# Two transformer blocks on one core: the 512- and the 256-column products of four weight blocks are issued in groups of one length

## The chip, the cores and the metric

One core of one Trainium2 chip runs the whole program. The metric is the device time of one execution in microseconds, the median of several runs. Before the change it is 2228.6 us (three runs, 2227.95 to 2229.66).

## What is computed

Two transformer blocks follow each other on 256 tokens of width 2048, batch 1, all in f32. The first mixes a gated short convolution, trailing means and a cross attention to 256 memory rows; the second has a dilated and a differential attention. Each ends in a gated feed-forward with an inner width of 5632. Nearly all of the arithmetic is products of the 256 tokens with weight matrices:

```python
h = rmsnorm(x, g_mix[l]);  z = h @ w_in[l]          # 2048 x 3584
... conv, trailing means, cross attention ...
x = x + mix @ w_out[l]                              # 2048 x 2048
u = causal_dwconv(rmsnorm(x, g_ffn[l]) @ w_up[l], ffn_conv_w[l]) + ffn_conv_b[l]   # 2048 x 11264
gate, val = jnp.split(u, 2, axis=-1)
x = x + (jax.nn.silu(gate) * val) @ w_down[l]       # 5632 x 2048
... second block: w_in_2 (2048 x 6144), two attentions, w_out_2, w_gate_2, w_up_2, w_down_2 ...
```

## The kernel before

Each f32 value is split into two parts of 12 bits, an upper one (`hi`) and a lower one (`lo`), and a product is made as three products of parts: upper by upper, upper by lower, lower by upper. The activations lie in SBUF as `[upper 256 tokens | lower 256 tokens]`, 512 columns per row tile of 128 (`A`, `hid`, `mix`, `y`, `M`). The weights come in blocks of 128 x 128. For one block, the upper part of the weights is loaded into TensorE and the 512 columns move past it; then the lower part is loaded and only the first 256 columns, the upper halves, move past that. These are the two products of this text: the one of 512 columns (line 200, and line 203 for the last block of an output tile) and the one of 256 (line 201). Both add to one PSUM tile `acc` of 512 columns, the short one to its upper half. Each product has a weight load of its own.

`product` (from line 198) issues the two products of one block. For all blocks but the last of an output tile the long one goes first; for the last it is the short one, so that the long one closes the sum:

```python
def product(acc, hi, lo, x, first, last):
    if not last:
        nc.tensor.matmul(acc, lhsT=hi, rhs=x, start=first, stop=False)
    nc.tensor.matmul(acc[:, S:], lhsT=lo, rhs=x[:, :S], start=False, stop=False)
    if last:
        nc.tensor.matmul(acc, lhsT=hi, rhs=x, start=False, stop=True)
```

The weights come from HBM in units of 16 blocks (1 MB each, line 185's `raw`), and a unit is taken in four quarters of four blocks. `emit_all` (line 977 on) goes through the quarters in order. In each it puts out, in this order: the load of the unit three ahead (first quarter), half a unit's `split_hi` on ScalarE (line 173) and `split_lo` on VectorE (line 185) for the units to come, the work that follows on finished output tiles (`post`), the quarter's products, and then small products such as attention scores (`extra`). The schedule is manual, so each engine takes its instructions in the order in which they are written. `ws_units` makes the units in which the weights stand still: its `emit` goes through the four blocks of a quarter and calls `product`. An output tile of 16 row tiles is 16 blocks, which is just a unit; in the feed-forward's second and third part an output tile of `w_down` has 14. `full_blocks` and `late_order` give the order of blocks: the first two output tiles of a matrix leave their last two row tiles until both have all else. The products of `w_k` at the start are written out by themselves, four output tiles side by side, and call `product` too.

In `vs_unit` (lines 242 to 244) it is the activations that stand still and 512 columns of weights that move. There all products have 512 columns, three for each pair of row tile and half of the tokens.

Of the kernel before, what the change touches and what calls it, by code (L numbers as in the profile page):

```python
# [18 lines left out]
P = 128  # L19
# [40 lines left out]
def late_order(ms, ks, late=2):  # L60
    """(output tile, row tile) in the order in which they are multiplied: the first two output tiles
    leave the last row tiles, which are made last, until both have all else."""
    ms, ks = list(ms), list(ks)
    if not late:
        return [(m, k) for m in ms for k in ks]
    both = [(m, k) for part in (ks[:-late], ks[-late:]) for m in ms[:2] for k in part]
    return both + [(m, k) for m in ms[2:] for k in ks]
# [32 lines left out]
def tile_two_blocks(ctx: ExitStack, tc: tile.TileContext, a: dict, out: bass.AP):  # L100
# [35 lines left out]
    def post(t, fn):  # L136
        """fn is called in quarter t of the units' time, before its products; a generator's
        further stages come a quarter later each."""
        posts.setdefault(t, []).append(fn)

    def extra(t, fn):
        """fn is called in quarter t, behind its products."""
        extras.setdefault(t, []).append(fn)
# [21 lines left out]
    def split_hi(j):  # L165
        """Half a unit's weights as two parts of 12 bits: the upper one."""
        i, second = divmod(j, 2)
        c0 = HB * second
        if i >= len(units) or c0 >= units[i][1]:
            return  # L170
        n = min(units[i][1] - c0, HB)
        hi = whi_p.tile([P, HB], F32R, tag="hi", name=f"hi{j}")
        nc.scalar.activation(hi[:, :n], raws[i][:, c0:c0 + n], AF.Copy)  # L173
        halves[j] = (hi, None)

    def split_lo(j):
        """The lower one."""
        i, second = divmod(j, 2)
        c0 = HB * second
        if i >= len(units) or c0 >= units[i][1]:  # L180
            return
        n = min(units[i][1] - c0, HB)
        hi = halves[j][0]
        lo = wlo_p.tile([P, HB], F32R, tag="lo", name=f"lo{j}")
        nc.vector.tensor_tensor(out=lo[:, :n], in0=raws[i][:, c0:c0 + n], in1=hi[:, :n].bitcast(F32), op=ALU.subtract)  # L185
        halves[j] = (hi, lo)
# [10 lines left out]

    def product(acc, hi, lo, x, first, last):
        if not last:
            nc.tensor.matmul(acc, lhsT=hi, rhs=x, start=first, stop=False)  # L200
        nc.tensor.matmul(acc[:, S:], lhsT=lo, rhs=x[:, :S], start=False, stop=False)  # L201
        if last:
            nc.tensor.matmul(acc, lhsT=hi, rhs=x, start=False, stop=True)  # L203

    def ws_units(src, blocks, done, ready=0):
        """Weights stand still, the halves of 256 tokens move together: blocks of (tile, moving, first,
        last) in order. The sums are in two parts: by upper halves alone, and the rest."""
        accs = {}
        for u in range(0, len(blocks), UB):
            part = blocks[u:u + UB]  # L210

            def emit(i, q, part=part):
                for b, (m, mov, st, sp) in list(enumerate(part))[4 * q:4 * q + 4]:
                    if st:
                        accs[m] = acc_p.tile([P, 2 * S], F32, tag="acc", name="acc")
                    hi, lo = weights(i, b * P, (b + 1) * P)
                    product(accs[m], hi, lo, mov(), st, sp)

            i = add_unit(src[u // UB], len(part) * P, emit)
            for b, (m, _, _, sp) in enumerate(part):  # L220
                if sp:
                    post(max(4 * i + b // 4 + 1, ready), lambda m=m: done(m, accs.pop(m)))
# [7 lines left out]
    def vs_unit(src, act, g, accs):  # L230
        """Activations stand still, 512 columns of weights move: the unit of row tiles 4g to 4g + 3."""
        def emit(i, b):
# [22 lines left out]
    def rsqrt_small(src, n, scale, eps):  # L255
        """1 / sqrt(src * scale + eps), by columns of a few elements."""
        v = sm.tile([P, n], F32, tag=f"rs_v{n}", name="rs_v")
# [11 lines left out]
    class Norm:  # L269
        """rms of the tokens: sums of squares by partition, then r (token on partitions) and  # L270
        R (token along the row, the same on each partition)."""

# [35 lines left out]
        def rows(self, dst, r):  # L308
            """r[token] from partitions to the free axis, on all partitions."""
            for t in range(2):  # L310
# [6 lines left out]
        def at(self, t):  # L317
            """The last x is added in quarter t; R is there for the posts of the quarter returned."""
            extra(t + 4, self.sums)
# [5 lines left out]
    class TwoNorms(Norm):  # L325
        """A norm of x whose gained result is normed again: r and R serve both together, R1 the first."""

# [30 lines left out]
    def put_act(kt, g, x, a, norm):  # L358
        """x with its gain to the halves of a, and x itself to the norm."""
        hi = a[:, kt, :S]  # L360
# [6 lines left out]
    def put_pair(hl, src, scale=None):  # L367
        """The halves of hl add up to src (times a column of scales), the first of 12 bits."""
        h = hl[:, :S]
# [10 lines left out]
    def whole(acc):  # L380
        """The two parts of the sums as one, to be had from the next stage on."""
        z = t1.tile([P, S], F32, tag="t", name="z")
# [10 lines left out]

    # ---- attention: one head's scores to probabilities to [d, token] or [token, d]
    def scores(q, k, parts=(slice(0, P),)):
# [6 lines left out]
    def softmax(src, scale, normalise=True):  # L402
        """src [P, 2, S]: exp(scale * (src - max)) and 1 / its sums."""
        mx = sm.tile([P, 2], F32, tag="mx", name="mx")
# [25 lines left out]
    def transposed(p):  # L430
        """[token, key] to PSUM [key, key tile, token]."""
        ps = m_p.tile([P, 2, S], F32, tag="m", name="pT_ps")
# [9 lines left out]

    # ---------------------------------------------------------------- constants and first loads
    stg = big.tile([P, KT + KT * S], F32, tag="stg", name="mem")
# [9 lines left out]
    def first_units():  # L454
        """Loads and splits of mem and of the first two units, in the order in which the products take them."""
        n = 4 * P
        for i in range(3):
            raws[i] = wraw_p.tile([P, UB * P], F32, tag="raw", name=f"raw{i}")
            for q in range(4):
                if i != 1:  # L460
                    load_mem(2 * i + q, 2 * i + q + 1)
                nc.sync.dma_start(raws[i][:, q * n:(q + 1) * n], units[i][0][:, q * n:(q + 1) * n])
        # The tensor engine's clock rises with use: it is kept busy until the first operands are there.
        warm = m_p.tile([P, 512], F32, tag="m", name="warm")
# [39 lines left out]

    # ---------------------------------------------------------------- block 1: keys and values of mem
    n_mem = Norm("mem")
# [41 lines left out]
    for g in range(4):  # L548
        vs_unit(a["w_v"][g], lambda: M, g, v_accs)

        def emit(i, b, g=g):
            kt = 4 * g + b
            if kt == 0:
# [3 lines left out]
                for _ in range(2):  # L557
                    ac = s_p.tile([P, 2 * S], F32, tag="s", name="acc_s")
                    k_accs.append(ac)
            for m in range(4):  # L560
                hi, lo = weights(i, (4 * b + m) * P, (4 * b + m + 1) * P)
                product(k_accs[m], hi, lo, M[:, kt, :], kt == 0, kt == KT - 1)

# [12 lines left out]

    # ---------------------------------------------------------------- block 1: mixer
    mix = {}
# [40 lines left out]

    # trailing means  # L620
    pooled_hl = {}
# [38 lines left out]

    # gated short convolution
    conv = {}
# [43 lines left out]

    # ---------------------------------------------------------------- residual stream
    def residual(gname, norm, scaled_to=None):
# [28 lines left out]

    # ---------------------------------------------------------------- gated feed-forward
    hid = {}
# [41 lines left out]

    # ---------------------------------------------------------------- block 2: attention
    vv = {}
# [174 lines left out]

    # ---------------------------------------------------------------- emission
    def finish():  # L960
# [46 lines left out]

# ---- layouts: [units, 128, columns], each unit's rows as the tensor engine takes them
def _blocks(w, order):
    """The 128 x 128 blocks of w [K, N] in the order of (row tile, column tile) given."""  # L1010
    k, n = w.shape
# [4 lines left out]
def _units(blocks):  # L1016
    """[blocks, 128, 128] as units of 16."""
    n = -len(blocks) % UB
# [5 lines left out]
def _rows(w):  # L1024
    """w [2048, n] as [128, 16, n]."""
    return np.ascontiguousarray(w.reshape(KT, P, -1).transpose(1, 0, 2))


def _moving(w):
    """w [2048, 512 * n]: for each 512 columns, four units of four row tiles."""  # L1030
    n = w.shape[1] // 512
    return np.ascontiguousarray(w.reshape(4, 4, P, n, 512).transpose(3, 0, 2, 1, 4)).reshape(-1, P, 4 * 512)
# [66 lines left out]
```

## Time and profile before

| | |
|---|---|
| median of 3 runs | 2228.6 us |
| the profiled execution | 2228.2 us from the first to the last instruction |
| TensorE products, share of the span | 2208.6 us, 99% |
| TensorE weight loads | 1912.5 us, 86% |
| VectorE, ScalarE, GpSimd | 72%, 51%, 5% |
| DMA | 409 MB, mean 184 GB/s |
| blocks with a 512 and a 256 product | 5774 |

The profile gives each product's start and a modelled end. Products overlap in the array, so the time that one product costs is read from its start to the start of the next one, and not from its duration. In this text a step is that distance. "Long" is a product of 512 columns and "short" one of 256; long-to-short is the step from the start of a long product to that of a short one behind it.

### The profile page before, as it was taken

The page shows a single profiled execution, that of the slowest core. Times are in us where ns is not written, and L with a number is a line of the kernel's source. Part 1 is how long each engine was busy: PE and PEld are TensorE (multiplying, and loading weights), DVE is VectorE, ACT ScalarE, POOL GpSimd, SP SyncE. Part 2 cuts the span into 40 slices and gives each one's busy share as a digit, 9 for nine tenths or more (in the row PEclk, how much of TensorE's full clock was granted, in tenths as well). Part 3 has the DMA queues.
Part 4 walks back from the last instruction along what each step waited for, and adds up shares of the span by engine and source line. Part 5 has one row for each costly group of instructions (what it writes and reads, how often), then busy time and mean ns, then how long its engine had stood idle before and what let it go on. Part 6 is the DMA issues. An engine that isn't in the chain of part 4 may idle for free.

```text
span 2228.2 us, 31353 instructions
## 1 busy us (share of the span) xinstructions
PE 2208.6 (99%) x12426; PEld 1912.5 (86%) x12426; DVE 1604.0 (72%) x2553; ACT 1145.1 (51%) x1738; POOL 105.9 (5%) x114
## 2 busy tenths in 40 slices
PE   8999999999999999999999999999999999999997
PEld 7888888888888888888888888888888888888886
DVE  8877778885588757878779677776665666666666
ACT  6555546554455535565456655454443444344442
POOL 4000010000000000003100000010000000000012
PEclk9999999999999999999999999999999999999998
DMA  7555555555555555555554444555555555555553
GB/s 276 200 170 178 185 184 191 187 189 189 189 185 182 186 184 189 189 189 184 189 169 158 163 159 154 186 189 189 184 180 187 189 187 189 189 189 185 184 183 111
DMA packets 60196, 409.00 MB, mean 184 GB/s; under 512 B 6672, under 2 KB 8592, under 8 KB 11792
## 3 DMA queue, kind: packets, MB, share of 16 engines
q1 hardware_dynamic: 60048, 406.99, 53.2%
q8 instruction: 97, 1.59, 0.3%
q14 instruction: 51, 0.42, 0.0%
HBM read 404.86 MB, written 2.10 MB: 183 GB/s over the span
## 4 chain that ended last, share of the span: by engine, by line
PE 97%; DVE 2%; DMA 1%; issue 0%; ACT 0%; DVEq 0%; SPq 0%; ACTq 0%
PE acc L200 56%; PE acc L201 30%; PE acc L203 4%; PE acc L242 1%; PE acc L243 1%; PE acc L244 1%; PE s_ps L399 1%; DMA raw<-in_w_k 1%; DVE lo L185 1%; PE pT_ps L435 0%; PE o_ps L890 0%; PE o_ps L848 0%; DVE A L364 0%; DVE end L968 0%; DVE M L512 0%; DMA mem<-in_mem 0%
## 5 line engine op out<-in xcount | busy, mean ns | idle before, releaser
L200 PE MATMUL acc<-A,hi 128*128 128x512 f32 x3540 | 1267.5, 400 | 0.0
L173 ACT ACTIVATE hi<-raw 128x1024 fp32r<-128x1024 f32 x758 | 800.0, 1057 | 590.5 <-PE acc L200 342.2
L185 DVE TENSOR_TENSOR lo<-raw,hi 128x1024 fp32r<-128x1024 f32 x758 | 932.3, 1237 | 156.4 <-ACT hi L173 144.8
L201 PE MATMUL acc<-A,lo 128*128 128x256 f32 x3776 | 1021.7, 281 | 0.0
L200 PEld LDWEIGHTS acc<-A,hi 128*128 128x128 f32 x3540 | 665.2, 188 | 152.8 <-issue 1.7
L201 PEld LDWEIGHTS acc<-A,lo 128*128 128x128 f32 x3776 | 712.9, 189 | 22.8
L200 PE MATMUL acc<-hid,hi 128*128 128x512 f32 x1312 | 464.9, 395 | 0.0
L201 PE MATMUL acc<-hid,lo 128*128 128x256 f32 x1408 | 380.0, 281 | 0.0
L200 PEld LDWEIGHTS acc<-hid,hi 128*128 128x128 f32 x1312 | 246.7, 188 | 53.9
L201 PEld LDWEIGHTS acc<-hid,lo 128*128 128x128 f32 x1408 | 264.1, 188 | 8.8
L383 ACT ACTIVATE z<-acc 128x256 f32<-128x256 f32 x244 | 92.6, 382 | 298.4 <-PE acc L203 298.1
L385 DVE TENSOR_TENSOR z<-acc,z 128x256 f32<-128x256 f32 x244 | 103.3, 423 | 123.4 <-ACT z L383 121.0
L710 DVE TENSOR_TENSOR X<-acc,X 128x256 f32<-128x256 f32 x128 | 54.1, 422 | 172.7 <-PE acc L203 172.7
L203 PE MATMUL acc<-A,hi 128*128 128x512 f32 x236 | 94.2, 399 | 0.0
L685 DVE SCALAR_TENSOR_TENSOR c<-z,vec,c 128x255 f32<-128x255 f32 (+1 forms) x188 | 90.1, 481 | 4.6 <-ACT c L680 0.7
L373 DVE TENSOR_TENSOR hid<-hid 128x256 fp32r<-128x256 f32 x88 | 37.4, 425 | 73.5 <-ACT hid L371 73.5
L200 PE MATMUL acc<-mix,hi 128*128 128x512 f32 x240 | 85.1, 395 | 0.0
L200 PE MATMUL acc<-y,hi 128*128 128x512 f32 x224 | 80.7, 397 | 0.0
L391 DVE TENSOR_TENSOR z<-z,R_ffn 128x256 f32<-128x256 f32 x176 | 74.8, 425 | 6.0
L201 PE MATMUL acc<-mix,lo 128*128 128x256 f32 x256 | 69.4, 281 | 0.0
L201 PE MATMUL acc<-y,lo 128*128 128x256 f32 x256 | 66.6, 281 | 0.0
L286 POOL TENSOR_TENSOR sq_attn<-sq_attn,sqt 128x256 f32<-128x256 f32 x30 | 29.4, 992 | 717.4 <-ACT sqt L284 717.3
(188 smaller groups left out, 1577.8 us busy)
## 6 DMA issues: line engine op xcount, KB each, us to landing
raw<-in_w_up SPq DMA_DIRECT2D x88, 1024.0 KB, 4.9
raw<-in_w_down SPq DMA_DIRECT2D x88, 1024.0 KB, 4.9
raw<-in_w_gu SPq DMA_DIRECT2D x88, 1024.0 KB, 4.9
raw<-in_w_out SPq DMA_DIRECT2D x32, 1024.0 KB, 4.9
raw<-in_w_in SPq DMA_DIRECT2D x22, 1024.0 KB, 4.8
raw<-in_w_qkb SPq DMA_DIRECT2D x16, 1024.0 KB, 4.8
raw<-in_w_qka SPq DMA_DIRECT2D x16, 1024.0 KB, 4.9
raw<-in_w_vb SPq DMA_DIRECT2D x8, 1024.0 KB, 4.9
```

The costliest lines, as they stand in the source:

```text
L173: nc.scalar.activation(hi[:, :n], raws[i][:, c0:c0 + n], AF.Copy)
L185: nc.vector.tensor_tensor(out=lo[:, :n], in0=raws[i][:, c0:c0 + n], in1=hi[:, :n].bitcast(F32), op=ALU.subtract)
L200: nc.tensor.matmul(acc, lhsT=hi, rhs=x, start=first, stop=False)
L201: nc.tensor.matmul(acc[:, S:], lhsT=lo, rhs=x[:, :S], start=False, stop=False)
L203: nc.tensor.matmul(acc, lhsT=hi, rhs=x, start=False, stop=True)
L286: nc.gpsimd.tensor_tensor(out=self.sq, in0=self.sq, in1=q, op=ALU.add)
L373: nc.vector.tensor_tensor(out=hl[:, S:], in0=src, in1=h.bitcast(F32), op=ALU.subtract)
L383: nc.scalar.activation(z, acc[:, S:], AF.Copy)
L385: nc.vector.tensor_tensor(out=z, in0=acc[:, :S], in1=z, op=ALU.add)
L391: nc.vector.tensor_tensor(out=d, in0=z, in1=R, op=ALU.mult)
L685: nc.vector.scalar_tensor_tensor(out=c[:, s:], in0=z[:, :S - s], scalar=w[2 - s], in1=c[:, s:], op0=ALU.mult, op1=ALU.add)
L710: nc.vector.tensor_tensor(out=dst, in0=acc[:, :S], in1=X[:, m, :], op=ALU.add)
```

## The change

`product` becomes `products`, which takes the four blocks of a quarter at once. It issues their long products together and their short ones together. A flag, kept from quarter to quarter, says which length the last quarter ended with, so that the next begins with the same one. A first block's long product stays ahead of its short one, since it clears the sum, and a last block's stays at the end, since it closes it. `ws_units` and the products of `w_k` call it. The number of products and their operands stay as they were. (Comments and descriptions are dropped elsewhere in the file, which changes nothing that runs.)

```diff
-    def product(acc, hi, lo, x, first, last):
-        if not last:
-            nc.tensor.matmul(acc, lhsT=hi, rhs=x, start=first, stop=False)
-        nc.tensor.matmul(acc[:, S:], lhsT=lo, rhs=x[:, :S], start=False, stop=False)
-        if last:
-            nc.tensor.matmul(acc, lhsT=hi, rhs=x, start=False, stop=True)
+    longs = [True]
+
+    def products(blocks):
+        mm = nc.tensor.matmul
+
+        def long(acc, hi, lo, x, first, last):
+            mm(acc, lhsT=hi, rhs=x, start=first, stop=last)
+
+        def short(acc, hi, lo, x, first, last):
+            mm(acc[:, S:], lhsT=lo, rhs=x[:, :S], start=False, stop=False)
+
+        opening = [b for b in blocks if b[4]]
+        closing = [b for b in blocks if b[5]]
+        between = [b for b in blocks if not b[4] and not b[5]]
+        if longs[0] and not closing:
+            for b in opening + between:
+                long(*b)
+            for b in blocks:
+                short(*b)
+            longs[0] = False
+        else:
+            for b in opening:
+                long(*b)
+            if opening and not closing:
+                for b in between:
+                    long(*b)
+            for b in blocks:
+                short(*b)
+            if not opening or closing:
+                for b in between:
+                    long(*b)
+            for b in closing:
+                long(*b)
+            longs[0] = bool(closing) or not opening
...
             def emit(i, q, part=part):
+                group = []
                 for b, (m, mov, st, sp) in list(enumerate(part))[4 * q:4 * q + 4]:
                     if st:
                         accs[m] = acc_p.tile([P, 2 * S], F32, tag="acc", name="acc")
-                    hi, lo = weights(i, b * P, (b + 1) * P)
-                    product(accs[m], hi, lo, mov(), st, sp)
+                    group.append((accs[m], *weights(i, b * P, (b + 1) * P), mov(), st, sp))
+                products(group)
...
-            for m in range(4):
-                hi, lo = weights(i, (4 * b + m) * P, (4 * b + m + 1) * P)
-                product(k_accs[m], hi, lo, M[:, kt, :], kt == 0, kt == KT - 1)
+            products([(k_accs[m], *weights(i, (4 * b + m) * P, (4 * b + m + 1) * P), M[:, kt, :],
+                       kt == 0, kt == KT - 1) for m in range(4)])
```

## Rows read from the trace of the kernel before

**Rows 1.** The page: busy time by engine, and TensorE's granted clock in 40 slices.

```profile
PE 2208.6 (99%) x12426; PEld 1912.5 (86%) x12426; DVE 1604.0 (72%) x2553; ACT 1145.1 (51%) x1738; POOL 105.9 (5%) x114
...
PEclk9999999999999999999999999999999999999998
```

**Rows 2.** The page: the chain that ended last, by engine and by line.

```profile
PE 97%; DVE 2%; DMA 1%; issue 0%; ACT 0%; DVEq 0%; SPq 0%; ACTq 0%
PE acc L200 56%; PE acc L201 30%; PE acc L203 4%; PE acc L242 1%; PE acc L243 1%; PE acc L244 1%; PE s_ps L399 1%; DMA raw<-in_w_k 1%; DVE lo L185 1%; PE pT_ps L435 0%; PE o_ps L890 0%; PE o_ps L848 0%; DVE A L364 0%; DVE end L968 0%; DVE M
```

**Rows 3.** Groups by line on PE: operation, operands, shapes, count, busy us, mean ns.

```profile
L200 PE MATMUL acc<-A,hi 128*128 128x512 f32 x3540 | 1267.5, 400 | 0.0
L201 PE MATMUL acc<-A,lo 128*128 128x256 f32 x3776 | 1021.7, 281 | 0.0
L200 PE MATMUL acc<-hid,hi 128*128 128x512 f32 x1312 | 464.9, 395 | 0.0
L201 PE MATMUL acc<-hid,lo 128*128 128x256 f32 x1408 | 380.0, 281 | 0.0
L203 PE MATMUL acc<-A,hi 128*128 128x512 f32 x236 | 94.2, 399 | 0.0
```

**Rows 4.** Waits of PE: who waited for whom, us in total, times, longest.

```profile
PE acc L243 <- DVE lo L185: 2.8, 2, 2.0
...
PE acc L201 <- DVE lo L185: 1.2, 2, 1.0
```

**Rows 5.** Timeline of PE, w_gu_2 (A moves): start us, duration us, operation, count.

```profile
1800.38 0.40 PE L201 MATMUL acc<-A,lo 128*128 128x256 f32 x2
1800.62 0.40 PE L203 MATMUL acc<-A,hi 128*128 128x512 f32 x1
1800.85 0.40 PE L200 MATMUL acc<-A,hi 128*128 128x512 f32 x1
1801.09 0.28 PE L201 MATMUL acc<-A,lo 128*128 128x256 f32 x1
1801.20 0.40 PE L200 MATMUL acc<-A,hi 128*128 128x512 f32 x1
...
1805.79 0.40 PE L200 MATMUL acc<-A,hi 128*128 128x512 f32 x1
```

**Rows 6.** Timeline of PE, w_down_2 (hid moves), one output tile and its start.

```profile
1693.22 0.40 PE L201 MATMUL acc<-hid,lo 128*128 128x256 f32 x2
1693.46 0.40 PE L203 MATMUL acc<-hid,hi 128*128 128x512 f32 x1
1693.70 0.39 PE L200 MATMUL acc<-hid,hi 128*128 128x512 f32 x1
...
1698.58 0.40 PE L200 MATMUL acc<-hid,hi 128*128 128x512 f32 x1
```

**Rows 7.** Timeline of PE: long products alone, from the last w_down product on.

```profile
1067.84 0.39 PE L203 MATMUL acc<-hid,hi 128*128 128x512 f32 x1
...
1069.92 0.40 PE L244 MATMUL acc<-hi,A 128*128 128x512 f32 x1
...
1071.29 0.39 PE L244 MATMUL acc<-hi,A 128*128 128x512 f32 x1
...
1074.69 0.39 PE L244 MATMUL acc<-hi,A 128*128 128x512 f32 x1
```

**Rows 8.** Timeline of PE: long products alone in w_v, where M stands still.

```profile
18.61 0.39 PE L242 MATMUL acc<-hi,M 128*128 128x512 f32 x1
...
22.11 0.40 PE L242 MATMUL acc<-hi,M 128*128 128x512 f32 x1
```

**Rows 9.** Timeline of PEld, w_down (weight loads beside the products of lines 200 and 201).

```profile
1000.01 0.19 PEld L201 LDWEIGHTS acc<-hid,lo 128*128 128x128 f32 x1
1000.25 0.19 PEld L200 LDWEIGHTS acc<-hid,hi 128*128 128x128 f32 x1
1000.37 0.19 PEld L201 LDWEIGHTS acc<-hid,lo 128*128 128x128 f32 x1
```

**Rows 10.** Timeline of PE: the last products with weights, ahead of the final norm.

```profile
2212.00 0.40 PE L201 MATMUL acc<-hid,lo 128*128 128x256 f32 x2
2212.23 0.40 PE L203 MATMUL acc<-hid,hi 128*128 128x512 f32 x1
```

## The prediction

> **What bounds the kernel now.** I read the page first: TensorE is busy 99% of the span at the full granted clock (2.4 GHz) in all but the last slice, and no other engine is above 72% [rows 1]. The chain of work that ended last agrees: 97% of it is TensorE, and lines 200, 201 and 203, the two products of each block, are 90% [rows 2]. The waits tell whether TensorE stands still for operands: it does so for the split weights in four places, 4.0 us in all, all in the first stages [rows 4]. So the time is the number of products times what each costs, and only the second factor can move: 5774 blocks, a long and a short product each (the groups of `A` and `hid` are the largest, 3540 and 1312 of line 200) [rows 3].
>
> A busy time says nothing here, since products overlap (a long one "lasts" 400 ns [rows 3]). What counts is the step from start to start, which the timeline gives. At 2.4 GHz, 512 columns are 213 ns and 256 are 107 ns, 320 ns a block. In the stage where `A` moves, 14 blocks take from 1800.85 to 1805.79, 352.9 ns a block [rows 5]; in a tile where `hid` moves, 14 blocks take 4.88 us, 348.6 ns [rows 6]. Over all alternating neighbours in the trace, without the few steps that hold a stall, long-to-short is 234.5 ns (5,318 of them) and short-to-long 117.7 (5,339): 352.2 ns a block. Some 32 ns a block, 9%, is lost between products, and this is all that the change can win from.
>
> **The change, part by part.** It removes and adds no instruction; it changes who follows whom. A tile of 16 blocks has 15 long-to-short and 15 short-to-long steps now, one short-to-short (the last two blocks) and one long-to-long (into the next tile). Afterwards the quarters run 4 long, 8 short, 8 long, 8 short, 4 long: two of each mixed step, 14 of each equal one. Counted over the block lists, with the shorter runs in tiles of 14, long-to-short falls from 5,324 to 779 and short-to-long as much; with `w_k` some 4,600 pairs of mixed steps become a long-to-long and a short-to-short. So
>
> change = 4,600 x (long-to-long + short-to-short - 352.2 ns).
>
> *Short-to-short.* It exists now, once at the end of each tile: two in 0.24, 0.24 and 0.23 us [rows 5, 6, 10], and over all 387 places 119.1 ns. It never stands in a row of eight, so I bound it: below by the shortest short step, 113 ns (1801.09 to 1801.20 [rows 5]), above by the longest, 124. I take 119.1, the same products in the same place.
>
> *Long-to-long.* Three kinds of rows. (a) From a tile's last long product to the next tile's first: 0.23 and 0.24 us [rows 5, 6], 234.6 ns over 364 places, but there a short one follows at once. (b) In a long row of long products where the activations stand still: 15 steps in 3.40 us, 226.7 ns, steady for hundreds of products [rows 7]. (c) The beginning of such a row, straight behind two short products: nine steps from 1067.84 to 1069.92, 231.1 ns; steps of 224 to 236 follow each other until, after some ten, the row settles at 226.7 [rows 7]. Where `M` stands still it never settles: 15 steps in 3.50 us, 233.3 ns [rows 8]; `M` lies in the buffer that `mix`, `hid` and `y` use later. Runs of eight between runs of short ones are most like (c), as they end before the row would have settled. I take 231, with 226.7 and 236 (the long step of the alternating stage) as ends.
>
> Sum: 231 + 119.1 = 350.1, which is 2.1 ns a pair less; times 4,600 it is 9.7 us. From the profiled execution's 2228.2 us that is 2218.5, and its span lies 0.4 us under the median. I say 2218 us.
>
> *Edits with no price.* The last long product of a tile stays last in its quarter, and the work on the sum is posted to the quarter behind it, so ScalarE and VectorE get it as before; where a tile of 14 ends inside a quarter, its close moves back by up to two or three products, 0.7 us, covered by four `acc` tiles. A short-first quarter needs its `lo` half up to 0.5 us earlier. `split_lo` is written a whole unit ahead, 5.6 us, and after the first stages TensorE never waits for it [rows 4]; without that cover it would cost those 0.5 us in each unit. The halves' buffers are set free by the same quarters, a product earlier or later, and the queue of loads on SyncE isn't passed by anything. In the first 60 us TensorE does wait for `lo` (1.2 us in line 201), where long-first may win and short-first lose a few tenths: within 2 us either way. The end, from the last product at 2212.23 [rows 10], keeps its order.
>
> [...]
>
> **The rivals.**
>
> *The long runs settle.* If, with equal neighbours, the row finds its steady spacing at once, long-to-long is 226.7 [rows 7], and 226.7 + 119.1 = 345.8, a gain of 6.4 x 4,600 = 29 us: 2199. If the short runs settle too, at their shortest 113, it is 340, 56 us: 2172. For it: 226.7 holds over hundreds of products with VectorE and ScalarE at work. Against: ten products of getting there, and 233.3 with `M`.
>
> *Nothing changes.* A product costs what its own length costs, with any loss moved to the next one. For it: in rows 5 a long step of 0.24 is followed by a short one of 0.11, as if one pays for the other, and short-to-short (119.1) is hardly different from short-to-long (117.7). Then the sum over a run is the same, 2228 within 4 us.
>
> *Slower: the runs of short products are held by their weight loads.* A load begins as a product begins (1000.01, 1000.25, 1000.37 [rows 9]), so one load is under way for each product, and a short product has hardly room for it: the loads of an alternating pair share 352 ns, while in a run of eight short ones each has only its own step. If nothing is won back in the long runs, that is 234.6 + 119.1 = 353.7, 7 us more: 2235. At the upper ends, 236 + 120 = 356, it is 2246; 124 would be 2264. It decides where long-to-long plus short-to-short exceeds 352.2, for instance above 233.1 with 119.1. For it: the nearest rows of the very same products say 353.7. Against: in (a) the second long product is followed by a short one, so it is no run.
> [...]
>
> That the change doesn't do what it says has little room: the order is manual, and TensorE takes its products as written.
>
> **How the numbers follow.** Forecast (gain between 5 and 19 us, from 232 to 229 ns of long-to-long): 0.42. Runs that settle (2205 and below): 0.17. Nothing: 0.23. Slower: 0.18. A measurement of this kernel tells some 0.2%, 4.5 us, from no change. So faster 0.59, same 0.23, slower 0.18. The likeliest case's own range is 2209 to 2224. The range of 8 in 10 goes on to the settled case with one length settled, 2190 (long 231 with short 113 is 2191), leaving out the case where both settle, and up to 2240, in the middle of the slower case: about 0.08 lies outside on either side.
>
> **What would show it.** In the trace after, a tile must show 4 long, 8 short, 8 long in a row; the step within a run of eight long ones should be near 231 ns, uneven at first, and within eight short ones near 119. A steady 226.7 from the third product on says the runs settle; short steps of 120 or more say the loads hold them. The count of long-to-short steps should be near 800, and TensorE's waits for `lo` should stay at some 4 us. The prediction is wrong if long-to-long is above 233 or if the short runs change by more than 2 ns, as each ns is 4.6 us.

## The result, and the profile after

The changed kernel takes 2204.6 us (median of 4 runs, 2203.8 to 2206.1) against 2228.9 us for the kernel before in the same comparison: a ratio of 0.989, 95% interval 0.988 to 0.991. It is 24 us faster. I had forecast faster, but by 10.6 us: the direction was right, and the size was not, as the gain is 2.3 times the forecast. The measured time lies inside the range from 2190 to 2240, in the part (2205 and below) that the prediction kept for runs that settle. The profiled execution's span falls from 2228.2 to 2202.7 us, 25.5 us.

The page after, by engine, by the chain that ended last, with TensorE's granted clock in the 40 slices, and with its largest group (line 206 is now the product of 512 columns, line 209 that of 256):

```profile
PE 2182.8 (99%) x12426; PEld 1909.5 (87%) x12426; DVE 1603.5 (73%) x2553; ACT 1143.2 (52%) x1738; POOL 106.7 (5%) x114
...
PEclk9999999999999999999999999999999999999998
...
PE 97%; DVE 1%; DMA 1%; issue 0%; SPq 0%; ACT 0%; DVEq 0%; ACTq 0%
...
L206 PE MATMUL acc<-A,hi 128*128 128x512 f32 x3776 | 961.6, 394 | 0.0
```

The bound is the same as in [rows 1, 2]: TensorE 99% busy at the same granted clock, 97% of the chain, the same 12426 products. TensorE waits no longer for the split weights than it did: 3.8 us, against 4.0 us in [rows 4]. Here are its waits for the lower halves, 3.6 us:

```profile
PE acc L274 <- DVE lo L185: 3.1, 2, 2.6
...
PE acc L274 <- DVE lo L507: 0.5, 2, 0.2
```

So the gain was made where the argument looked for it, between the products. The timeline of PE shows the runs, each merged to one row (start, duration, count). First a stage in which `A` moves, to be set against [rows 5], then one in which `hid` moves, against [rows 6]:

```profile
402.52 2.00 PE L206 MATMUL acc<-A,hi 128*128 128x512 f32 x8
404.36 1.12 PE L209 MATMUL acc<-A,lo 128*128 128x256 f32 x8
405.31 2.00 PE L206 MATMUL acc<-A,hi 128*128 128x512 f32 x8
407.15 1.12 PE L209 MATMUL acc<-A,lo 128*128 128x256 f32 x8
```

```profile
540.78 1.07 PE L209 MATMUL acc<-hid,lo 128*128 128x256 f32 x8
541.68 1.99 PE L206 MATMUL acc<-hid,hi 128*128 128x512 f32 x8
543.51 1.11 PE L209 MATMUL acc<-hid,lo 128*128 128x256 f32 x8
544.46 2.00 PE L206 MATMUL acc<-hid,hi 128*128 128x512 f32 x8
```

Eight long products are followed by eight short ones, as planned. With `A`, eight long ones take 1.84 us (230 ns each) and eight short ones 0.95 (119). With `hid`, the long ones take 1.83, but the short runs differ by turns: 0.90 us (113 ns each) and 0.95 (119). Before the change single steps of 113 ns occur, but no short run at 113 is in any row read from that trace.

All steps of the two traces (mean ns, count). Left out are 69 steps before and 64 after, most of them in the stages with attention, that are over 260 ns behind a long product or over 140 behind a short one:

| step | before | after | after, `A` moves | after, `hid`, `mix`, `y`, `M` move |
|---|---|---|---|---|
| long-to-long | 234.6 (364) | 230.3 (4908) | 230.8 | 229.4 |
| short-to-short | 119.1 (387) | 117.9 (4937) | 118.7 | 116.2 |
| long-to-short | 234.5 (5321) | 228.6 (785) | 227.8 | 229.9 |
| short-to-long | 117.7 (5339) | 118.3 (786) | 119.6 | 116.2 |

Within a run the place matters. Where `A` moves, the long steps of a run of eight are, in the mean, 233, 235, 229, 232, 231, 227, 227, 227 ns and the short ones 114, 118, 120, 120, 120, 120, 120, 120. So a long run is uneven for five products and then settles at 227. The row of [rows 7] comes to the same 227 by another way: its steps go up and down between 224 and 236 for the first eleven. Where `hid` moves, the long steps mostly go round 226, 229, 232 and the short ones stay at 113 or at 118 for the whole run.

### The profile page after: what moved, and what is told of

Its sections match the earlier page's. It is cut to its first block, busy times and chain, and to the rows that moved or that the text cites. A ratio compares the mean times of both kernels' runs of the same rounds, so it can differ in the third digit from the quotient of the medians.

```text
span 2202.7 us, 31334 instructions
## 1 busy us (share of the span) xinstructions
PE 2182.8 (99%) x12426; PEld 1909.5 (87%) x12426; DVE 1603.5 (73%) x2553; ACT 1143.2 (52%) x1738; POOL 106.7 (5%) x114
## 4 chain that ended last, share of the span: by engine, by line
PE 97%; DVE 1%; DMA 1%; issue 0%; SPq 0%; ACT 0%; DVEq 0%; ACTq 0%
PE acc L206 60%; PE acc L209 31%; PE acc L273 1%; PE acc L274 1%; PE acc L275 1%; PE s_ps L430 1%; DVE lo L185 0%; DMA X<-in_x 0%; PE pT_ps L466 0%; PE o_ps L920 0%; PE o_ps L878 0%; DMA raw<-in_w_k 0%; DVE end L998 0%; PE nps L342 0%; PE o_ps L638 0%
## 5 line engine op out<-in xcount | busy, mean ns | idle before, releaser
L206 PE MATMUL acc<-A,hi 128*128 128x512 f32 x3776 | 961.6, 394 | 0.0
L206 PEld LDWEIGHTS acc<-A,hi 128*128 128x128 f32 x3776 | 677.3, 189 | 119.8 <-issue 1.0
L209 PEld LDWEIGHTS acc<-A,lo 128*128 128x128 f32 x3776 | 518.5, 190 | 39.2 <-issue 0.7
L209 PE MATMUL acc<-A,lo 128*128 128x256 f32 x3776 | 535.0, 283 | 0.0
L206 PE MATMUL acc<-hid,hi 128*128 128x512 f32 x1408 | 360.2, 392 | 0.0
L209 PEld LDWEIGHTS acc<-hid,lo 128*128 128x128 f32 x1408 | 195.3, 188 | 17.2
L209 PE MATMUL acc<-hid,lo 128*128 128x256 f32 x1408 | 199.6, 279 | 0.0
L740 DVE TENSOR_TENSOR X<-acc,X 128x256 f32<-128x256 f32 x128 | 54.0, 422 | 177.4 <-PE acc L206 177.3
L206 PE MATMUL acc<-mix,hi 128*128 128x512 f32 x256 | 64.2, 392 | 0.0
L392 ACT ACTIVATE A<-X,vec 128x256 fp32r<-128x256 f32 x64 | 32.4, 507 | 57.8 <-DVE X L741 57.3
L741 DVE TENSOR_TENSOR X<-acc,X 128x256 f32<-128x256 f32 x128 | 54.3, 424 | 4.4
L395 DVE SCALAR_TENSOR_TENSOR A<-X,vec,A 128x256 fp32r<-128x256 f32 x64 | 50.6, 802 | 8.3 <-ACT A L392 8.3
```

What stands on the lines that cost most here:

```text
L206: mm(acc, lhsT=hi, rhs=x, start=first, stop=last)
L209: mm(acc[:, S:], lhsT=lo, rhs=x[:, :S], start=False, stop=False)
L395: nc.vector.scalar_tensor_tensor(out=a[:, kt, S:], in0=x, scalar=g, in1=hi.bitcast(F32), op0=ALU.mult, op1=ALU.subtract)
L740: nc.vector.tensor_tensor(out=dst, in0=acc[:, :S], in1=X[:, m, :], op=ALU.add)
L741: nc.vector.tensor_tensor(out=dst, in0=acc[:, S:], in1=dst, op=ALU.add)
```

## The experiments

Three theories were set against each other.

- Theory 1: a run of equal products settles, and its steps depend on the place in the run.
- Theory 2: each pair of changes of length has a fixed price, some 5.3 ns.
- Theory 3: the steps follow from the distance in SBUF between the rows that move and the weights, modulo some hundred bytes. The distance is how far the rows begin behind the weights. In each partition, the rows of `A` begin 32 bytes past a multiple of 512, those of the buffer of `M`, `mix`, `hid` and `y` 96 past it, and the upper and lower weight halves both 32 past it. So `A` is at distance 0 from the weights, and the other buffer at 64.

Each comparison ran beside the kernel before, which gave 2228.7 to 2229.8 us.

**Longer runs.** Eight blocks in a group instead of four, so that runs have 16 products:

```diff
             def emit(i, q, part=part):
+                if q % 2 == 0:
+                    return
                 group = []
-                for b, (m, mov, st, sp) in list(enumerate(part))[4 * q:4 * q + 4]:
+                for b, (m, mov, st, sp) in list(enumerate(part))[4 * q - 4:4 * q + 4]:
...
-                    post(max(4 * i + b // 4 + 1, ready), lambda m=m: done(m, accs.pop(m)))
+                    post(max(4 * i + 2 * (b // 8) + 2, ready), lambda m=m: done(m, accs.pop(m)))
```

> The changed kernel, but eight blocks instead of four are taken as one group, so that runs are 16 products of one length instead of 8; pairs of mixed steps fall from 787 to 449. Theory 1 (a run has to settle: where A moves, the long steps of a run of eight are 233, 235, 229, 233, 231, 227, 227, 227 ns, the short ones 114, 118 and then 120): the products 9 to 16 of a run go on with 227 and 120 ns where A moves, the mean long step there falls from 230.2 to about 228.6 and the short one rises from 118.9 to 119.4; the whole is 2200 us against the changed kernel's 2204.6. Theory 2 (each change of length costs a fixed price, 24 us over 4,600 pairs taken away, 5.3 ns each): 338 pairs fewer are 1.8 us, 2203, and the steps within a run don't depend on their place.

It took 2201.2 us (ratio 0.988, 0.986 to 0.989), 3.4 us less than the changed kernel. The total alone would hardly tell 2200 from 2203. The trace does:

```profile
404.58 2.08 PE L209 MATMUL acc<-A,lo 128*128 128x256 f32 x16
406.49 3.82 PE L206 MATMUL acc<-A,hi 128*128 128x512 f32 x16
```

The sixteen short ones take 1.91 us, 119.4 ns each, as theory 1 said. Over all runs with `A`, the long steps 9 to 16 are 226.7 ns and the short ones 120.0. The mean long-to-long step with `A` falls to 228.9, and the short-to-short one rises to 119.4. The place in the run counts, and there is no fixed price for a change of length.

**All of it 32 bytes further.** Before and after the change the rows began at odd multiples of 32 bytes. One constant tile made 32 bytes longer moves weights and moving rows alike:

```diff
-    ones = cst.tile([P, P], F32, name="ones")
+    ones = cst.tile([P, P + 8], F32, name="ones")[:, :P]
```

> The changed kernel with one tile of constants 32 bytes longer, so that all weight halves and moving rows lie 32 bytes further: they began 32 bytes past a multiple of 512 (A and the weights) and 96 past one (hid, mix, y), and now begin 64 and 128 past it, each on a multiple of 64; their distance to each other is as before. Theory 3 (the spacing follows from where the moving rows begin relative to the weight blocks): nothing changes, 2204.6 within 2 us. Rival, absolute alignment: rows that begin on a multiple of 64 lose less; if the whole 13 ns by which a settled long step (226.7) exceeds its 213 ns of columns were that, 5774 long steps would give 75 us.

2205.0 us (0.989, 0.988 to 0.991): no change from 2204.6, and long-to-long with `A` stays at 230.8. A start on a multiple of 64 bytes brings nothing, as long as the distance stays.

**`A` moved by 64 bytes against the weights.** The buffer behind it is padded so that its own distance stays at 64:

```diff
-    X = big.tile([P, KT, S], F32, name="X")
+    X = big.tile([P, KT * S + 16], F32, name="X")[:, :KT * S].rearrange("p (k t) -> p k t", k=KT)
...
-    stg = big.tile([P, KT + KT * S], F32, tag="stg", name="mem")
+    stg = big.tile([P, KT + KT * S + 112], F32, tag="stg", name="mem")[:, :KT + KT * S]
```

> The changed kernel with A moved by 64 bytes, so that its rows begin 96 bytes past a multiple of 512 as those of hid, mix and y do, while the weights (32 past it) and hid stay (modulo 512). Theory 3 (the distance between moving rows and weight blocks sets the pattern): where A moves the steps become those of hid, long-to-long from 230.8 to 229.4 ns and short-to-short from 118.7 to 116.2, over 3,700 blocks some 14 us: 2190 us. Theory 1 alone (only the place in the run counts): 2204.6, with the steps in the stages of A unchanged.

2192.5 us (0.984, 0.982 to 0.985), 12 us less than the changed kernel for 64 bytes of nothing. The stages with `A` now show the two kinds of short runs that only `hid` had, 0.90 and 0.95 us:

```profile
404.09 1.07 PE L209 MATMUL acc<-A,lo 128*128 128x256 f32 x8
404.99 1.99 PE L206 MATMUL acc<-A,hi 128*128 128x512 f32 x8
406.82 1.11 PE L209 MATMUL acc<-A,lo 128*128 128x256 f32 x8
407.77 2.00 PE L206 MATMUL acc<-A,hi 128*128 128x512 f32 x8
```

The mean steps with `A` become 229.0 and 115.9 ns, those of `hid` (229.4 and 116.2). Theory 1 alone would have left them at 230.8 and 118.7. The same trace shows it once more where `A` stands still and the weights move: the steps there, 228.0 ns in the mean at distance 0, become 233.3.

**The reverse: the other buffer at distance 0.** Only the second of the two edits above, so that the buffer of `hid` moves by 448 bytes:

> The changed kernel with the buffer of M, mix, hid and y moved by 448 bytes, so that its rows begin 32 bytes past a multiple of 512, at distance 0 from the weight blocks, as those of A do; A stays. The reverse of the run that moved A. Theory 3 (distance sets the pattern): where hid, mix and y move, the short steps in a run become 114, 118, 120, 120 ... and the long ones 233, 235, 229, 233, 231, 227 ..., a block there costs 349.2 ns as in the run with products alone, against 345.6 in the changed kernel; over some 1,980 blocks that is 7 us more: 2212 us. Theory 1 alone (place in the run): 2204.6.

2211.2 us (0.992, 0.990 to 0.994), 6.5 us more, as worked out. Now both short runs of a tile take as long with `hid` too, 0.95 and 0.96 us; the mean step is 118.7 ns:

```profile
541.92 1.11 PE L209 MATMUL acc<-hid,lo 128*128 128x256 f32 x8
542.87 2.00 PE L206 MATMUL acc<-hid,hi 128*128 128x512 f32 x8
544.71 1.11 PE L209 MATMUL acc<-hid,lo 128*128 128x256 f32 x8
545.67 1.55 PE L206 MATMUL acc<-hid,hi 128*128 128x512 f32 x6
```

And where `M` stands still, the long products alone, which kept at 233 ns in [rows 8], now settle at 227 after about a dozen.

**The alternating kernel with `A` moved.** Both edits above on the kernel before the change:

> The kernel before, alternating as it was, with A moved by 64 bytes as in the run of the changed kernel that gained 12 us. In the run with products alone, alternating blocks cost 353.3 ns at distance 0 and at 64. Theory 3 in its full form (distance and order act together): nothing or little is gained here, 2222 (if A's stages take the mean of hid's, 351.1 against 352.7) to 2229 us. Rival: distance 64 is simply the better place, whatever the order; then the same 12 us are gained, 2216.

2224.3 us (0.998, 0.997 to 0.999), 5 us less than before the change. With `A`, long-to-short goes from 235.8 to 232.0 ns and short-to-long from 116.9 to 119.2, to the 232.0 and 119.1 of `hid`. So the same move of `A` is worth 12 us in the grouped order and 5 in the alternating one: the address and the order act together.

**Products alone.** To see the steps without the rest, a kernel with nothing but products, 48 long and 48 short ones in several orders at several distances. Apart from ScalarE, which copies a sum out at the end of each segment, no other engine works meanwhile:

```python
for n, (kind, b) in enumerate(order):            # order: alternating, groups of four or eight, one kind alone
    w = slice(wb // 4 + b % 8 * P, wb // 4 + (b % 8 + 1) * P)
    c = mb // 4 + b % 16 * 2 * S
    ...
    if kind == "L":
        nc.tensor.matmul(acc, lhsT=hi[:, w], rhs=mv[:, c:c + 2 * S], start=st, stop=sp)
    else:
        nc.tensor.matmul(acc[:, S:], lhsT=lo[:, w], rhs=mv[:, c:c + S], start=st, stop=sp)
```

> Only products, no model: it leaves the whole computation of the reference out. 12 pairs of byte offsets (weights, moving rows, past a multiple of 512), and for each 48 long and 48 short products in five orders: alternating, runs as in the change from groups of four blocks and of eight, then 48 long ones alone and 48 short ones alone. Nothing else uses SBUF at the time. Theory 3: offsets of equal distance are alike, (32,32) as (0,0), and (32,96) as (0,64); alternating blocks cost some 353 ns at distance 0 and 349 to 353 at 64; short ones alone 120 at distance 0 and 113 or 118 at 64. Theory 1: at distance 0 long ones alone settle at 226.7 within ten products. Theory 2: the order costs the same at all distances. If VectorE, ScalarE and DMA traffic in SBUF were the cause of the loss, all orders would come out below the kernel's steps here.

Here are groups of four blocks, that is runs of eight products, at distance 0, from the timeline of PE:

```profile
45.88 2.00 PE L61 MATMUL acc<-mv,hi 128*128 128x512 f32 x8
47.72 1.12 PE L63 MATMUL acc<-mv,lo 128*128 128x256 f32 x8
48.68 2.00 PE L61 MATMUL acc<-mv,hi 128*128 128x512 f32 x8
50.52 1.12 PE L63 MATMUL acc<-mv,lo 128*128 128x256 f32 x8
```

These are the rows of the model's stage with `A`, to 0.01 us. In all, from one execution (ns a block, or a product where one kind is alone; the first products of each segment left out). In brackets stand the bytes past a multiple of 512 at which weights and moving rows begin:

| distance, bytes | alternating | groups of four | long alone | short alone |
|---|---|---|---|---|
| 0 (32 and 32, or 0 and 0) | 353.3 | 349.2 | 226.7 | 120.0 |
| 64 (32 and 96, or 0 and 64) | 353.3 | 344.6 | 228.9 | 117.8 |
| 32 | 346.7 | 350.8 | 233.2 | 116.7 |
| 96 | 350.0 | 353.3 | 233.4 | 119.8 |
| 128 (also 384) | 351.1 | 351.2 | 232.1 | 118.6 |
| 192 | 353.3 | 346.9 | 233.4 | 113.3 |
| 16 | 360.0 | 347.5 | 231.5 | 113.3 |
| 480 (32 and 0) | 353.5 | 351.7 | 233.3 | 118.4 |

Distance 0 gives the 353 ns of [rows 5] and the 349 ns of the stages with `A` after the change; distance 64 gives the 345 ns of `hid` after it. Distances that differ by 256 are alike (0 and 256, 128 and 384). The work of VectorE, ScalarE and DMA isn't needed for the loss, since it is there, and as large, without them. And the order that is quicker depends on the distance: in groups of four a block costs 4.1 ns less at 0, 8.7 less at 64, but 4.1 more at 32 and 3.3 more at 96.

**One distance for the upper weight halves, another for the lower.**

> Products alone, the computation of the reference left out: 48 long ones, and 48 short ones, at each distance from 0 to 240 bytes in steps of 16; then alternating and grouped blocks with one distance for the upper weight halves and another for the lower ones. Theory 3: long ones are quickest at distance 0 (226.7), short ones where the first such run showed 113.3 (16 and 192). If the two lengths act apart, a pair with 0 for the upper and 192 for the lower half gives some 226.7 + 113.3 = 340 ns a block in long runs, plus what the settling of the long runs costs (3.5 ns a block in runs of eight): 343 to 344, below the 344.6 of distance 64. If a step follows from both loads that stand beside it, the mixed pairs come out elsewhere.

Alone, long products were quickest at 0 (226.7 ns), then at 16 (228.3, where the run before had 231.5) and 64 (228.9). Short ones lay between 116.7 and 120.1 at all 16 distances. The 113.3 of the run before didn't return (117.4 at 16 and 117.8 at 192), so a short run can hold more than one spacing at the same distance, as with `hid`; the distance alone doesn't fix the step. The pair 0 and 192 gave 347.5 ns in groups of four and 343.9 in groups of eight. Its short runs alone had 117.8 and not 113.3, so 226.7 + 117.8 + 3.5 = 348.0 was to be expected for the lengths acting apart, and the pair doesn't decide that question. The next one does. The surprise was the pair 64 for the upper and 0 for the lower half: its lengths alone cost 228.9 and 120.0, 348.9 together, and in groups of four a block costs 348.3, but in the alternating order it is 340.0, the least of all. The reversed pair, 0 and 64, alternating, costs 351.1. The stretch of alternating products, with 40 blocks between the second row and the last, 13.60 us:

```profile
565.77 0.39 PE L64 MATMUL acc<-mv,hi 128*128 128x512 f32 x1
566.00 0.28 PE L66 MATMUL acc<-mv,lo 128*128 128x256 f32 x1
...
579.37 0.39 PE L64 MATMUL acc<-mv,hi 128*128 128x512 f32 x1
579.60 0.28 PE L66 MATMUL acc<-mv,lo 128*128 128x256 f32 x1
```

**That pair in the two kernels.** 64 bytes ahead of the lower halves, and the buffers behind padded to match, in the kernel before and in the changed one:

```diff
+    pad_p = pool("pad", 1)
     wlo_p = pool("wlo", 4)
...
+    pad = pad_p.tile([P, 16], F32, name="pad")
...
-    stg = big.tile([P, KT + KT * S], F32, tag="stg", name="mem")
+    stg = big.tile([P, KT + KT * S + 112], F32, tag="stg", name="mem")[:, :KT + KT * S]
...
         nc.vector.memset(ones, 1.0)
+        nc.gpsimd.memset(pad, 0.0)
```

> The kernel before, in its alternating order, with 64 bytes put ahead of the lower weight halves and the moving buffers placed to match: the rows of A, hid, mix and y begin 64 bytes behind the upper halves and 0 behind the lower ones (modulo 256). With products alone, alternating blocks at this pair of distances cost 340.0 ns, the least of all that were run. Theory 3 (each step is set by the distance between the rows that move and the weights that are being loaded beside them, so order and addresses act together): 12.2 ns a block less than 352.2, 5774 blocks, 70 us, of which some 2 go back in the products where activations stand still: 2160 us. Rival (alternating the length is itself what costs, as the change supposes): no better than 2224, as when only A was moved. If VectorE, ScalarE and DMA break up the steady spacing, somewhere between.

> The changed kernel, in groups, at the same placement (64 behind the upper, 0 behind the lower weight halves). With products alone, groups of four blocks cost 348.3 ns there. Theory 3: 348.3 against the 348.0 of the changed kernel as it was, so 2204 to 2210 us, some 45 us slower than the alternating order at the same addresses: the change would be a loss of 2% there. Rival (equal neighbours are better in themselves): the grouped order is still the quicker of the two.

The alternating kernel: 2172.4 us (0.975, 0.973 to 0.976). The grouped one: 2208.6 us (0.991, 0.989 to 0.992). At these addresses the very change of this case would cost 36 us. The alternating one fell 12 us short of what I expected. Its timeline, around the end of one tile and to the end of the next:

```profile
402.31 0.40 PE L203 MATMUL acc<-A,lo 128*128 128x256 f32 x2
402.54 0.39 PE L205 MATMUL acc<-A,hi 128*128 128x512 f32 x1
402.77 0.39 PE L202 MATMUL acc<-A,hi 128*128 128x512 f32 x1
403.00 0.28 PE L203 MATMUL acc<-A,lo 128*128 128x256 f32 x1
403.12 0.39 PE L202 MATMUL acc<-A,hi 128*128 128x512 f32 x1
403.35 0.28 PE L203 MATMUL acc<-A,lo 128*128 128x256 f32 x1
403.47 0.39 PE L202 MATMUL acc<-A,hi 128*128 128x512 f32 x1
...
407.55 0.39 PE L202 MATMUL acc<-A,hi 128*128 128x512 f32 x1
```

From 403.47 to 407.55 there are 12 blocks, 340 ns each, with all the other engines at work. What is lost against 340 ns a block shows at the tile's end, where the last block is turned round (short, short, long, long): some 27 ns each time.

**The alternation kept up through a tile's end.** The kernel before at the same placement, with this edit in addition:

```diff
-        if not last:
-            nc.tensor.matmul(acc, lhsT=hi, rhs=x, start=first, stop=False)
-        nc.tensor.matmul(acc[:, S:], lhsT=lo, rhs=x[:, :S], start=False, stop=False)
-        if last:
-            nc.tensor.matmul(acc, lhsT=hi, rhs=x, start=False, stop=True)
+        nc.tensor.matmul(acc, lhsT=hi, rhs=x, start=first, stop=False)
+        nc.tensor.matmul(acc[:, S:], lhsT=lo, rhs=x[:, :S], start=False, stop=last)
```

> The alternating kernel at the placement of 64 and 0 bytes, with long then short in the last block of a tile too, so that nothing breaks the alternation at a tile's end. In the run at that placement the steps are 227 and 113 ns through each tile, and around each of the 387 ends 122, 229, 231, 120, 232 instead of 113, 227, 227, 113, 227: 27 ns each, 10.5 us. Theory 3: 2162 us. Rival: the start of a new tile (another PSUM bank, the first row again) is what disturbs the spacing; then it stays at 2172.

2163.0 us (0.970, 0.969 to 0.972): 67 us less than the kernel before it, and 42 less than the changed one. The start of a new tile disturbs nothing; the turned block did. A stretch that is longer than a tile of 16 blocks:

```profile
401.74 0.39 PE L201 MATMUL acc<-A,hi 128*128 128x512 f32 x1
401.97 0.28 PE L202 MATMUL acc<-A,lo 128*128 128x256 f32 x1
402.08 0.39 PE L201 MATMUL acc<-A,hi 128*128 128x512 f32 x1
402.31 0.28 PE L202 MATMUL acc<-A,lo 128*128 128x256 f32 x1
...
407.52 0.39 PE L201 MATMUL acc<-A,hi 128*128 128x512 f32 x1
```

17 blocks in 5.78 us: 340 ns. Over the whole trace long-to-short is 226.8 ns (5708 steps) and short-to-long 113.5 (5703).

## Where the prediction was right, and which step failed

*The bound.* Right: the time lay in TensorE's steps, its waits for the split weights stayed at some 4 us, and nothing else set the pace. The count was right too: 5321 long-to-short steps became 785, against 5,324 and 779 by the block lists outside `w_k`.

*The sum.* It was one product, 4,600 x (231 + 119.1 - 352.2), and it came out at 9.7 us. With the measured steps the gain has these terms:

| term | forecast, us | measured, us |
|---|---|---|
| pairs of mixed steps exchanged, at the forecast prices (4,600 forecast, 4,540 measured) | 9.7 | 9.5 |
| their long-to-long at 230.3 instead of 231 | 0 | 3.2 |
| their short-to-short at 117.85 instead of 119.1 | 0 | 5.7 |
| 785 long-to-short steps that stay, 228.6 instead of 234.5 | 0 | 4.6 |
| 786 short-to-long steps that stay, 118.3 instead of 117.7 | 0 | -0.5 |
| the 364 and 387 equal steps that were there already | 0 | 2.1 |
| the 69 and 64 longer steps (9.8 to 8.0 us beyond the mean step) | 0 | 1.8 |
| sum | 9.7 | 26.4 |

The span fell by 25.5; the other 0.9 us was lost in steps beside the small products.

*The step that failed.* It is the sum: its price for short-to-short, and the steps that it left at their old cost. I took 119.1 for short-to-short, "the same products in the same place", from runs of two. With `A` that was nearly right (118.7). With the other buffer it was 116.2, since about half of the runs there hold 113. I had 113 as the lower bound, as the shortest single step of the alternation, but no row of before shows a run at it, and I gave it no part in the likeliest case. By the prediction's own sign, a change of the short runs by more than 2 ns, it was wrong where `hid` moves (2.9 ns), though not over all (1.2). The experiments show what sets the difference: moving `A` by 64 bytes takes its short runs from 118.7 to 115.9, and moving the other buffer to distance 0 takes its own from 116.2 to 118.7.

The second failure is a term that I left out: I priced every mixed step that stays at its old cost. But a long-to-short step at the end of a long run isn't the long-to-short step of an alternation. It is the last step of a run that has settled, 227 to 228 ns with `A`, and the steps already equal fell with it. A change of neighbours reprices all the steps, not only the exchanged ones. Long-to-long itself, the term on which I spent most words, was right within 0.7 ns, but in part by luck: row (c) of [rows 7] has the mean of the new runs with `A` (231.1 against 230.8), not their sequence, since it is uneven for eleven products and they for five; and with the other buffer the step is 229.4. The gain hangs on a difference of a few ns a pair: 2.1 was forecast, 4.0 measured.

*A gap without neighbours.* The Trainium skill, TensorE: Matmul & The Clock Gate, Back-to-back issue gap, gives columns at 2.4 GHz plus 2.5 ns as the gap of an isolated product, and says that in a stream of weight loads and products both set the spacing. From that gap a block would cost 325 ns in any order, an estimate. No order or distance here came below 340.0, and order alone moved a block by up to 12.5 ns (360.0 to 347.5 in groups of four at distance 16). So the isolated gap is no price for these streams.

*The rivals.* "The long runs settle" is half of what happened: with `A` they do, from the sixth product on, and the run with groups of eight shows it to the end of the run; with `hid` they circle round 229. "Nothing changes" fell. "The short runs are held by their weight loads" fell in this kernel: the short runs became shorter, not longer. As I had put it, with 119 to 120 ns against 117.7, it is what a short run at distance 0 does: its steps settle at the 120 that the prediction named as a sign of the loads. But the long steps win back more, and no run shows that the loads are the reason.

*What the prediction didn't see.* It treated the order as the cause. The runs show that order and placement act together: with the addresses of this kernel grouping gains 24 us, with `A` 64 bytes further it gains 32 (2224.3 to 2192.5), with 64 and 0 it loses 36 (2172.4 to 2208.6). The rows could have hinted at it: [rows 5, 6] show the same two products at 352.9 and 348.6 ns a block in tiles that move different buffers (over all steps the difference is smaller, 352.7 and 351.1), and [rows 7, 8] long products alone at 226.7 and 233.3. I used these as ends of a range, and didn't ask what made them differ. The runs answer it for the second pair: the weights that move past `M` begin 64 bytes ahead of it, which is 192 modulo 256, and at 192 long products alone cost 233.4 ns; at 0, 226.7.

*What stays open.* Why the distance matters isn't shown. The best pair fits one reading: while a product moves, the weights of the next are loaded [rows 9]. In the alternation at 64 and 0, a long product has a lower half loaded beside it, at distance 0, where long products alone are quickest as well; a short one has an upper half beside it, at 64. That would be two streams of reads from SBUF that meet or miss each other. It isn't shown, and in its simplest form, where each step costs what it costs alone at the distance of the load beside it, the same run speaks against it: alternating, 0 and 192 would cost 353.4 ns and 192 and 64 would cost 346.7; they cost 346.7 and 353.3. The Trainium skill, TensorE: Matmul & The Clock Gate, Step-by-step: what each phase is for, says that moving rows and weight loads have SBUF read ports of their own, so that a load takes no bandwidth from a running product; the runs with products alone speak against taking this as no influence at all, as in the alternating order only addresses differ between 340.0 and 360.0 ns. Nor is it shown why a short run holds 113 in one case and 118 in the next.

## What to carry to other kernels

Read the step from start to start, by buffer and by place in a run, before pricing an exchange of neighbours; and reprice every step that gets a new neighbour, also those that the change leaves alone. Where two groups of the same instruction differ by their operands' buffers alone, ask for their addresses: here 64 bytes of padding (and 448 that keep the other buffer in step), with the order that suits them, were worth 67 us, and the reordering by itself 24. Try order and placement together, in a kernel of products alone: it gave the cost of a block in the whole kernel to about 1 ns (2 ns for `hid` in the alternating order, 353.3 against 351.1).

## What was not expected of the hardware

The spacing of products depends on the distance in SBUF between moving rows and weights. Distances that differ by 256 bytes gave the same (0 with 256 and 128 with 384 were compared). The same 96 products, alternating, cost from 340.0 to 360.0 ns a block at 2.4 GHz. The best steady steps were 226.7 ns for 512 columns and 113.3 for 256, both 17/16 of 512 and 256 cycles at 2.4 GHz (213.3 and 106.7 ns), and both were held through whole tiles with all engines at work. Some sequences have more than one steady spacing at the same distance: short runs at distance 64 stay at 113 or at 118 ns as long as they last.
